# A partial tap sum and the layer norm's last mean read from PSUM instead of SBUF

## The chip, the cores and the metric

The kernel runs on one core of a Trainium2 chip. A time is the device time of one execution in microseconds (us), as the median of several runs. The engines are named as in the profile: PE is TensorE, DVE is VectorE, ACT is ScalarE, POOL is GpSimd, SP issues the loads. SBUF is the large on-chip memory, PSUM the small one of 8 banks (each 128 partitions by 512 f32) into which PE writes.

## The reference

A trunk of two layers on 512 tokens of 1024 channels, all in f32. The change lies in the second layer, a causal depthwise convolution followed by a layer norm:

```
u, g, xq, gate = split(h @ conv_w_in)               # 1536, 1536, 512, 2048 channels
glu = u * sigmoid(g)
y[t] = dw_b + sum over k of dw_w[k] * glu[t - 30 + k]   # 31 taps, per channel
y = silu(layernorm(y, ln_g, ln_b))                  # over the 1536 channels
x = x + rmsnorm((concat(y, memory_attention(xq)) * silu(gate)) @ conv_w_out) * norm_post_g
```

## The kernel before

Channels lie on the partitions and tokens on the free axis, so a tile is 128 channels by 512 tokens, and the convolution has 12 tiles (`NB`). Every product of the projections is done three times (high and low parts of both operands, lines 252 to 254, `split3`). The weights arrive in units of 128x1024: SP loads one into `wraw`, ACT casts it to `whi` (line 179), and DVE (line 183) or POOL (line 186, in two halves) subtracts to get the remainder `wlo`. Which of the two does it is fixed by the unit's number.

Every engine runs its instructions in the order in which the program emits them. `weave()` emits the chunks of a projection for PE and puts other work between them at given positions; it does not look at time. A product tile of u and g is left in two banks of the pool `mm` (4 banks); line 1037 takes the sigmoid on ACT and line 1038 multiplies on DVE into `gl`, which frees the banks for PE.

The taps: ahead of DVE's turn at a tile, ACT multiplies some of its taps (line 1063, into `pr`) and POOL sums them into `part` in SBUF (line 1064). That happens for 10 of the 12 tiles. DVE takes the remaining taps (line 1077), with the running sum in a PSUM bank of the pool `acc` (2 banks). Its first instruction for a tile multiplies `gl` by a tap and adds `part`; both tensors are in SBUF. The later ones add the bank `acc`. DVE works on two tiles in turn.

The layer norm: the mean of the first 8 tiles is taken off every tile early (line 1150). At the end `ln_sums` makes, on PE, the row of the sum of squares (line 1232) and the sum of the remaining differences on all partitions (line 1233); ACT scales the latter to a mean `es` in SBUF (line 1236); DVE makes the variance row (lines 1238, 1241) and takes `es` off the tiles (line 1247, `centre`): three tiles at once, the other nine one by one. PE turns the variance row into columns (line 1252), POOL takes the power -1/2 (lines 332, 335), DVE makes diagonals (line 340), PE spreads them (line 346). Then, per tile: centre, times the reciprocal deviation from PSUM (line 1267), silu on ACT (line 1268), times the gate (line 1274, both tensors in SBUF), high part on ACT (line 698), remainder on POOL (line 699). Two tiles make one of the units 2 to 7 of the output projection's first half, which PE runs meanwhile.

Of the kernel before, what the change touches and what calls it, by code (L numbers as in the profile page):

```python
# [58 lines left out]
def _turns(p):  # L59
    from fractions import Fraction  # L60

    # 1 / (2 pi) to 200 bits, by Machin's formula on integers
    one = 1 << 260

    def atan_inv(n):
        t = one // n
        s, k, sign = t, 3, -1
        while t:
            t //= n * n
            s += sign * (t // k)  # L70
            sign, k = -sign, k + 2
        return s

    pi = 4 * (4 * atan_inv(5) - atan_inv(239))
    f = Fraction((1 << p) * one, 2 * pi)
    f -= f.__floor__()
    if f > Fraction(1, 2):
        f -= 1
    c1 = round(f * 2**12) / 2.0**12
    r = f - Fraction(c1)  # L80
    c2 = round(r * 2**24) / 2.0**24
    c3 = float(r - Fraction(c2))
    q = 2.0**-p
    return c1 * q, c2 * q, c3 * q
# [7 lines left out]
def trunk(ctx, tc, x, x_t, mem_t, pos, g_cols, w_mem, post_g, w0, w1, dw_w, dw_b,  # L92
# [34 lines left out]
    ones = gp.tile([P, P], F32, name="ones")  # L127
    nhalf = gp.tile([P, 8], F32, name="nhalf")
# [9 lines left out]
    nc.gpsimd.memset(ones, 1.0)  # L138
    nc.gpsimd.dma_start(out=inv, in_=c_inv)
# [5 lines left out]
    # ------------------------------------------------------------------  # L145
    # weight stream: raw -> hi (float32r) and the exact remainder lo
    # ------------------------------------------------------------------
    units = [w_mem[i] for i in range(8)]
    units += [w0[i] for i in range(w0.shape[0])]
    # of the last product's second half, the first two units come early, then again  # L150
# [7 lines left out]
    def send(upto):  # L158
        """loads of the units before upto; a raw tile is free once its unit is split"""
        for i in range(sent["dma"], min(upto, sent["conv"] + 3, nu)):  # L160
            raws[i] = gp.tile([P, 2, G], F32, tag="wraw", bufs=3, name=nm("wraw"))
            src = units[i].rearrange("p (k c) -> p k c", k=2)
            for ks in (slice(0, 1), slice(1, 2)) if i == 0 else (slice(0, 2),):
                nc.sync.dma_start(out=raws[i][:, ks], in_=src[:, ks])
            sent["dma"] = i + 1
# [25 lines left out]
    def prefetch():  # L191
        """five split units at a time: those held, in use and ahead"""
        n = sent["use"]
        base = min(held) if held else n - 1
        conv_units(min(n + sent["ahead"], base + 5))
        send(sent["conv"] + 3)
# [14 lines left out]
    # ------------------------------------------------------------------  # L211
    # Every engine runs in the order of emission: weave() puts pieces of other work between
    # the chunks of a projection, where their operands are ready, and fill() work that only
    # other engines than the tensor engine do.
    # ------------------------------------------------------------------
# [40 lines left out]
    def proj(hT, tok_major, evac, n=S):  # L256
        """chunks of a group of 512 columns; evac(a, psum) as accumulator a is done"""
# [23 lines left out]
    def proj_halves(hT, evac, tok_major=False):  # L281
        """the same, the first half of the tokens before the second"""
# [37 lines left out]
    def rstd_two(ss):  # L320
        """of a row of D elements, from the sums of squares of its two halves"""
        v, w, r = tiny([P, 1]), tiny([P, 1]), tiny([P, 1])
        nc.gpsimd.tensor_scalar(out=v, in0=ss[:, 0:1], scalar1=1.0 / D, scalar2=EPS,
                                op0=ALU.mult, op1=ALU.add)
        nc.gpsimd.tensor_scalar(out=w, in0=ss[:, 1:2], scalar1=1.0 / D, scalar2=v,  # L325
                                op0=ALU.mult, op1=ALU.add)
        nc.gpsimd.tensor_tensor(out=r, in0=w, in1=nhalf[:, 0:1], op=ALU.pow)
        return r
# [15 lines left out]
    def spread(dg, sp):  # L344
        """column values -> the same along the free axis on every partition, from diags()"""
        nc.tensor.matmul(sp[:, :dg.shape[-1]], ones, dg, start=True, stop=True)
        return sp
# [11 lines left out]
    def split_T(pt, kp, gcol, dst):  # L359
        """transposed tiles (two of channels, two of tokens), times the gain, split"""  # L360
# [29 lines left out]
    # ------------------------------------------------------------------  # L390
    # start: loads ([channel, token]), warm-up of the tensor engine, memory keys and values
    # (the row scale of the memory's norm comes after the products)
    # ------------------------------------------------------------------
# [21 lines left out]
    def split_c(src, kp, gcol, dst):  # L415
        """channel tiles 2 kp and 2 kp + 1, times the gain, split"""
# [10 lines left out]
    def squares(key, xt):  # L427
        """of [channel, token], summed over the channel tiles"""
# [11 lines left out]
    def col_rstd(keys):  # L440
        """one column per tile of tokens"""
# [43 lines left out]
    # ------------------------------------------------------------------  # L485
    # memory attention: scores and softmax, transposes, gated output (split, [channel, token])
    # ------------------------------------------------------------------
    def xattn(xq, gx, yx, rs=None):
        """rs: what the scores of a token are scaled by, if not by SCALE alone"""
# [66 lines left out]
        def sides(at):  # L556
            """at[t]: chunks of the scores, the transposes and the output of tile t"""
# [8 lines left out]
    def part_of(sides, n):  # L566
        """those of group n of 16 chunks"""
        return [(pos_ - 16 * n, fn, cost) for pos_, fn, cost in sides if pos_ // 16 == n]
# [7 lines left out]
    # ------------------------------------------------------------------  # L576
    # output projection, post-norm and residual
    # ------------------------------------------------------------------
    def out_proj(yT, layer, res, finish, junk, sides, mids=()):
        """yT(j): split [channel, token] operand number j in stream order"""  # L580
# [4 lines left out]
        # the last tile of tokens ends with columns 512..767, then 768..1023, in two banks  # L585
# [118 lines left out]
    # ==================================================================  # L704
    # layer 0: retention
    # ==================================================================
    with tc.tile_pool(name="l0", bufs=1) as lp:
# [6 lines left out]
        def rope_tables():  # L714
            """in steps"""
# [15 lines left out]
            def rnd(o, i, scale):  # L731
                """nearest integer of i * scale"""
# [62 lines left out]
        # --- memory attention of layer 0 and the values, [token, channel]  # L795
# [4 lines left out]
        # the row scale of the norm comes after the products here as well  # L800
# [216 lines left out]
    # ==================================================================  # L1017
    # layer 1: convolution
    # ==================================================================
    with tc.tile_pool(name="l1", bufs=1) as lp:  # L1020
# [22 lines left out]
        # Taps 0..n-1 of a tile go to the scalar engine and GpSimd, which sum them ahead of the  # L1043
        # vector engine's turn; it then takes the others.
# [3 lines left out]
        def product():  # L1048
            """a tap on the scalar engine, summed by GpSimd; false if there is none to take"""
# [17 lines left out]
        def tap_sum(ct, k, first):  # L1067
            """a tap on the vector engine"""
            if first:
                accs[ct] = acc_ps()  # L1070
            gl, ac, tap = gls[ct], accs[ct], taps[:, ct, k:k + 1]
            o = cy[:, ct, :] if k == CW - 1 else ac
            if k == 0:
# [4 lines left out]
                out=o, in0=gl[:, k:k + S], scalar=tap,  # L1078
                in1=parts[ct] if first else ac, op0=ALU.mult, op1=ALU.add)

        def tap_sums(g):
            """the vector engine's turn at pair g"""
# [6 lines left out]
        def merge(a, b, stop=0.9):  # L1089
            """b spread over a, up to the fraction stop of it"""  # L1090
# [8 lines left out]
        # second half of the tokens of the layer's input, behind the first products  # L1099
# [12 lines left out]
        # Layer norm over channels (partitions and tiles).  The mean m0 of the first NM tiles  # L1112
        # serves as the shift: with d = y - m0 and e = mean(d), the centred d - e is what the
        # norm scales, and mean(d^2) - e^2 is its variance (e^2 is at most a third of mean(d^2),
        # as only 4 of 12 tiles can move the mean off m0).
# [3 lines left out]
        def gather(key, tile_):  # L1119
            """running sum on GpSimd"""  # L1120
# [108 lines left out]
        def ln_sums():  # L1229
            el, vr = tp_ps(), tp_ps()  # L1230
            for i, sq in enumerate([ln["dsums"]] + ln["sq"]):
                nc.tensor.matmul(vr[0:1, :], ones[:, 0:1], sq, start=i == 0, stop=i == 2)
            nc.tensor.matmul(el, ones, ln["d2"], start=True, stop=True)
            # var * BW = sum(d^2) - BW * e^2, as a row, then one column per tile of tokens
            es = ln["es"] = w2("m0", 1)
            nc.scalar.mul(out=es, in_=el, mul=1.0 / BW)
            e2 = w2("pr", PR)
            nc.vector.scalar_tensor_tensor(out=e2[0:1, :], in0=es[0:1, :], scalar=-float(BW),
                                           in1=es[0:1, :], op0=ALU.mult, op1=ALU.mult)
# [9 lines left out]
        def ln_cols():  # L1249
            vcol = tp_ps()  # L1250
# [42 lines left out]
        def norm_of(a, b):  # L1293
            """the steps of the norm that fall in chunks a..b-1 from the last gate's first"""
# [19 lines left out]
def _units(w, cols):  # L1314
    """[K, N] -> per group of 512 columns, per pair of K tiles: [128, 2 * 512]"""
# [61 lines left out]
```

## Time and profile before

| | |
|---|---|
| time, median of 3 runs | 844.36 us (843.94 to 844.42) |
| span of the profiled execution | 841.7 us |
| PE busy | 810.2 us, 96% |
| DVE busy | 526.8 us, 63% |
| POOL busy | 425.7 us, 51% |
| ACT busy | 347.7 us, 41% |

The profiled execution's own time is its span of 841.7 us; the median of the runs also holds what lies around the first and the last instruction, 2.7 us. Busy shares are means over the whole span: in the page's slices from about 505 to 715 us DVE is busy nine tenths of the time or more (the convolution). PE is the engine to look at first: 31.5 us of the span are without a matmul.

### The profile page before, as it was taken

To read this page: it belongs to the slowest core of one execution; us is meant where nothing else is said; L and a number is where in the kernel's file an instruction comes from. 1 tells how busy PE (TensorE), PEld (TensorE's weight loads), DVE (VectorE), ACT (ScalarE), POOL (GpSimd) and SP (SyncE) were. 2 spreads that over 40 slices of the span, in tenths; PEclk is the share of its full clock that TensorE was granted. 3 is DMA by queue.
4 is the path that set the end of the run, shared out by engine and by line. 5 is a ranking of instruction groups with operands and counts; after the bars stand their busy time and mean duration, and the time that the engine had idled before them with its cause. 6 is when DMAs were issued, how large, how long until landed. Compare 5 with 4: busy or idle time off the path is not lost.

```text
span 841.7 us, 10426 instructions
## 1 busy us (share of the span) xinstructions
PE 810.2 (96%) x3904; PEld 677.3 (80%) x3904; DVE 526.8 (63%) x814; ACT 347.7 (41%) x559; POOL 425.7 (51%) x380
## 2 busy tenths in 40 slices
PE   8999999999999999999999999979999989989897
PEld 8878888888888888888888988868877878766686
DVE  5797121143674642432337589999999999769523
ACT  6753356422112132332326352724678653335511
POOL 2145433356566564000043459988986898367101
PEclk9999999999999999999999999999999999999899
DMA  7722222222213112324423232222221124211522
GB/s 266 259 96 100 100 76 71 77 91 91 85 51 107 56 65 92 120 100 161 140 100 126 76 124 101 77 100 76 100 75 51 51 76 133 92 51 50 198 78 100
DMA packets 24961, 84.97 MB, mean 101 GB/s; under 512 B 2976, under 2 KB 4512, under 8 KB 24656
## 3 DMA queue, kind: packets, MB, share of 16 engines
q1 hardware_dynamic: 24256, 83.90, 28.8%
q8 instruction: 30, 0.49, 0.2%
q10 hardware_dynamic: 432, 0.21, 0.1%
q0 software_dynamic: 224, 0.21, 0.1%
q14 instruction: 19, 0.16, 0.1%
HBM read 80.11 MB, written 4.19 MB: 100 GB/s over the span
## 4 chain that ended last, share of the span: by engine, by line
PE 75%; DVE 14%; ACT 4%; DMA 3%; issue 2%; POOL 2%; SPq 0%; POOLq 0%; DVEq 0%; ACTq 0%
PE mm L252 21%; PE mm L253 21%; PE mm L254 21%; DVE acc L1077 6%; DMA wraw<-in_w_mem 2%; DVE cy L1274 1%; DVE cy L1247 1%; PE acc L919 1%; ACT whi L179 1%; PE tp L543 1%; PE tp L500 1%; DVE cy L1150 1%; DVE wlo L183 1%; PE tp L900 1%; PE acc L921 1%
## 5 line engine op out<-in xcount | busy, mean ns | idle before, releaser
L186 POOL TENSOR_TENSOR wlo<-wraw,whi 128x512 fp32r<-128x512 f32 x184 | 243.6, 1350 | 237.4 <-ACT whi L179 221.6
L252 PE MATMUL mm<-big,whi 128*128 128x512 f32 (+1 forms) x608 | 236.7, 389 | 10.3 <-DVE gl L1038 4.7
L254 PE MATMUL mm<-big,wlo 128*128 128x512 f32 (+1 forms) x608 | 229.2, 377 | 0.2 <-DVE wlo L176 0.2
L253 PE MATMUL mm<-big,whi 128*128 128x512 f32 (+1 forms) x608 | 228.9, 376 | 0.0
L1077 DVE SCALAR_TENSOR_TENSOR acc<-gl,taps,acc 128x512 f32<-128x512 f32 x282 | 188.5, 744 | 0.0
L179 ACT CAST whi<-wraw 128x1024 fp32r<-128x1024 f32 x133 | 137.1, 1047 | 89.6 <-PE mm L254 32.2
L254 PE MATMUL mm<-whi,big 128*128 128x512 f32 (+1 forms) x432 | 168.1, 389 | 2.0 <-POOL big L699 2.0
L252 PE MATMUL mm<-whi,big 128*128 128x512 f32 (+1 forms) x408 | 162.6, 398 | 0.0
L253 PE MATMUL mm<-wlo,big 128*128 128x512 f32 (+1 forms) x408 | 157.8, 387 | 0.2 <-DVE wlo L183 0.2
L252 PEld LDWEIGHTS mm<-big,whi 128*128 128x128 f32 x608 | 116.3, 191 | 31.1 <-DVE gl L1038 5.2
L254 PEld LDWEIGHTS mm<-big,wlo 128*128 128x128 f32 x608 | 116.2, 191 | 21.6 <-DVE wlo L176 0.6
L253 PEld LDWEIGHTS mm<-big,whi 128*128 128x128 f32 x608 | 116.2, 191 | 18.8 <-issue 0.5
L254 PEld LDWEIGHTS mm<-whi,big 128*128 128x128 f32 x432 | 81.5, 189 | 20.7 <-POOL big L699 3.9
L253 PEld LDWEIGHTS mm<-wlo,big 128*128 128x128 f32 x408 | 76.8, 188 | 15.5 <-DVE wlo L183 0.7
L252 PEld LDWEIGHTS mm<-whi,big 128*128 128x128 f32 x408 | 76.7, 188 | 14.5 <-issue 0.2
L183 DVE TENSOR_TENSOR wlo<-wraw,whi 128x1024 fp32r<-128x1024 f32 x41 | 54.5, 1344 | 41.9 <-ACT whi L179 41.8
L1064 POOL TENSOR_TENSOR part<-part,pr 128x512 f32<-128x512 f32 x56 | 72.5, 1317 | 6.1 <-ACT pr L1063 6.1
L892 ACT ACTIVATE kz<-tp,zeta 128x384 f32<-128x384 f32 x8 | 4.7, 584 | 96.5 <-PE tp L890 96.5
L1063 ACT ACTIVATE pr<-gl,taps 128x512 f32<-128x512 f32 x56 | 38.5, 717 | 1.8 <-POOL part L1064 1.8
L503 DVE TENSOR_REDUCE tiny<-tp 128x2 f32<-128x512 f32 x16 | 10.9, 684 | 27.0 <-PE tp L500 27.0
L325 POOL TENSOR_SCALAR tiny<-tiny,tiny 128x1 f32<-128x1 f32 x11 | 3.0, 271 | 41.1 <-ACT pr L600 34.6
L959 DVE TENSOR_TENSOR vb<-vb,ra 128x512 f32<-128x512 f32 x12 | 8.3, 691 | 24.0 <-ACT ra L957 24.0
(219 smaller groups left out, 904.1 us busy)
## 6 DMA issues: line engine op xcount, KB each, us to landing
wraw<-in_w SPq DMA_DIRECT2D x126, 512.0 KB, 3.3
wraw<-in_w_mem SPq DMA_DIRECT2D x7, 512.0 KB, 4.7
big<-in_x_t SPq DMA_DIRECT2D x2, 1024.0 KB, 7.5
o<-in_x SPq DMA_DIRECT2D x1, 2048.0 KB, 8.8
x1d<-o SPq DMA_DIRECT2D x4, 512.0 KB, 2.7
o<-x1d SPq DMA_DIRECT2D x1, 2048.0 KB, 10.2
out<-o SPq DMA_DIRECT2D x3, 512.0 KB, 2.6
big<-in_mem_t SPq DMA_DIRECT2D x4, 256.0 KB, 6.3
```

The costliest lines, as they stand in the source:

```text
L179: nc.scalar.copy(out=hi, in_=raw)
L183: nc.vector.tensor_tensor(out=lo, in0=raw, in1=hi.bitcast(F32), op=ALU.subtract)
L186: nc.gpsimd.tensor_tensor(out=lo[:, k], in0=raw[:, k], in1=hi[:, k].bitcast(F32), op=ALU.subtract)
L252: nc.tensor.matmul(dst, lh, rh, start=start, stop=False)
L253: nc.tensor.matmul(dst, lh, rl, start=False, stop=False)
L254: nc.tensor.matmul(dst, ll, rh, start=False, stop=stop)
L500: nc.tensor.matmul(sc[:, j * M:(j + 1) * M], xq[:, h, t * P:(t + 1) * P], mkT[:, h, :], start=True, stop=True)
L503: nc.vector.reduce_max(out=mx[:, hs], in_=sc.rearrange("p (a b) -> p a b", a=2), axis=AX.X)
L543: nc.tensor.matmul(po[:, h * P:(h + 1) * P], mv[:, m, h * P:(h + 1) * P], pT[:, m, h, :], start=m == 0, stop=m == 1)
L1063: nc.scalar.activation(out=pr, in_=gl[:, k:k + S], func=AF.Copy, scale=tap)
L1064: nc.gpsimd.tensor_tensor(out=parts[ct], in0=parts[ct], in1=pr, op=ALU.add)
L1077: nc.vector.scalar_tensor_tensor(out=o, in0=gl[:, k:k + S], scalar=tap, in1=parts[ct] if first else ac, op0=ALU.mult, op1=ALU.add)
```

## The change

Three edits. First, where a tile has a partial sum from POOL, a DVE copy of `part` into the tile's PSUM bank is put ahead of DVE's first tap, and that tap then adds the bank like all others. Second, the sum of differences is made with a matrix that holds 1/1536 instead of ones (`mean_of`, one more memset on POOL at the start), so PE writes the mean itself into PSUM; ACT's scaling of 128 rows becomes a copy of one row, needed because the variance uses the mean twice; `centre` reads the mean from PSUM. Third, the banks: the mean holds a bank of the pool `tp` (2 banks) until the last tile is centred, and the row of squares and the variance columns go to the pool `acc`. The diff also removes comments, which shifts line numbers.

```diff
+    mean_of = gp.tile([P, P], F32, name="mean_of")
...
     nc.gpsimd.memset(ones, 1.0)
+    nc.gpsimd.memset(mean_of, 1.0 / BW)
...
             if first:
                 accs[ct] = acc_ps()
+                if k:
+                    nc.vector.tensor_copy(out=accs[ct], in_=parts[ct])
...
             nc.vector.scalar_tensor_tensor(
-                out=o, in0=gl[:, k:k + S], scalar=tap,
-                in1=parts[ct] if first else ac, op0=ALU.mult, op1=ALU.add)
+                out=o, in0=gl[:, k:k + S], scalar=tap, in1=ac, op0=ALU.mult, op1=ALU.add)
...
         def ln_sums():
-            el, vr = tp_ps(), tp_ps()
+            es, vr = tp_ps(), acc_ps()
...
-            nc.tensor.matmul(el, ones, ln["d2"], start=True, stop=True)
-            es = ln["es"] = w2("m0", 1)
-            nc.scalar.mul(out=es, in_=el, mul=1.0 / BW)
-            e2 = w2("pr", PR)
+            nc.tensor.matmul(es, mean_of, ln["d2"], start=True, stop=True)
+            ln["es"] = es
+            e1, e2 = w2("m0", 1), w2("pr", PR)
+            nc.scalar.copy(out=e1[0:1, :], in_=es[0:1, :])
             nc.vector.scalar_tensor_tensor(out=e2[0:1, :], in0=es[0:1, :], scalar=-float(BW),
-                                           in1=es[0:1, :], op0=ALU.mult, op1=ALU.mult)
+                                           in1=e1[0:1, :], op0=ALU.mult, op1=ALU.mult)
...
         def ln_cols():
-            vcol = tp_ps()
+            vcol = acc_ps()
```

On DVE, where its turn at the second pair of tiles with a partial sum begins (`part` is POOL's sum, `acc` the PSUM bank, `gl` the gated input), the order before is:

```order
L1077 SCALAR_TENSOR_TENSOR cy<-gl_4038,taps,acc_4270 128x512
L1077 SCALAR_TENSOR_TENSOR acc_4590<-gl_4211,taps,part_4274 128x512
L1077 SCALAR_TENSOR_TENSOR acc_4592<-gl_4234,taps,part_4292 128x512
L1038 TENSOR_TENSOR gl_4600<-mm_4435,gl_4600 128x512
L1077 SCALAR_TENSOR_TENSOR acc_4590<-gl_4211,taps,acc_4590 128x512
```

And at the same place with the change:

```order
L1081 SCALAR_TENSOR_TENSOR cy<-gl_4040,taps,acc_4272 128x512
L1074 COPY acc_4594<-part_4278 128x512
L1081 SCALAR_TENSOR_TENSOR acc_4594<-gl_4213,taps,acc_4594 128x512
L1074 COPY acc_4597<-part_4296 128x512
L1081 SCALAR_TENSOR_TENSOR acc_4597<-gl_4236,taps,acc_4597 128x512
L1040 TENSOR_TENSOR gl_4606<-mm_4439,gl_4606 128x512
```

Two copies come in; the multiply that frees PE's banks (line 1038, now 1040) stays behind both first taps.

On DVE in the layer norm, from the variance row on (`m` is the mean in SBUF, `tp` a PSUM bank), before:

```order
L1238 SCALAR_TENSOR_TENSOR pr_6040<-m_1020_6038 1x512
L1241 TENSOR_TENSOR pr_6042<-tp_6033,pr_6040 1x512
L1247 TENSOR_TENSOR cy<-cy,m_1020_6038 128x512 x3
L1255 COPY tiny_6071<-tp_6066 128x4
L340 TENSOR_SCALAR pr_6103<-ident,tiny_6075 128x128 x4
L1267 TENSOR_TENSOR cy<-cy,tp_6108 128x512 x2
L1274 TENSOR_TENSOR cy<-cy,big_5353 128x512
```

And with the change:

```order
L1241 SCALAR_TENSOR_TENSOR pr_6051<-tp_6044,m_1020_6050 1x512
L1244 TENSOR_TENSOR pr_6054<-acc_6045,pr_6051 1x512
L1250 TENSOR_TENSOR cy<-cy,tp_6044 128x512 x3
L1258 COPY tiny_6083<-acc_6078 128x4
L342 TENSOR_SCALAR pr_6115<-ident,tiny_6087 128x128 x4
L1270 TENSOR_TENSOR cy<-cy,tp_6120 128x512 x2
L1277 TENSOR_TENSOR cy<-cy,big_5363 128x512
```

Nothing moves here; the operands change their memory.

## Rows read from the trace of the kernel before

**Rows 1.** Waits of PE, whole span: us in total, times, longest us

```profile
PE mm L252 <- DVE gl L1038: 4.7, 1, 4.7
PE mm L252 <- ACT whi L179: 3.3, 1, 3.3
PE mm L252 <- ACT big L1217: 2.8, 1, 2.8
PE tp L346 <- DVE pr L340: 2.7, 1, 2.7
PE mm L254 <- POOL big L699: 2.0, 3, 0.7
...
PE mm L253 <- DVE wlo L183: 1.6, 2, 1.3
```

**Rows 2.** Stretches of PE: from:to, us, busy (matmuls), granted clock, DMA

```profile
567.00:572.20 5.20, 5.17 (x12) 0.51 0.01 3
572.20:580.00 7.80, 7.80 (x36) 1.00 0.19 67
746.35:753.00 6.65, 6.64 (x20) 0.76 0.23 79
783.50:788.00 4.50, 4.42 (x12) 0.59 0.67 204
```

**Rows 3.** DVE's groups by form: count, busy us, mean ns, idle before

```profile
L1077 DVE SCALAR_TENSOR_TENSOR acc<-gl,taps,acc 128x512 f32<-128x512 f32 x282 | 188.5, 744 | 0.0
...
L1077 DVE SCALAR_TENSOR_TENSOR acc<-gl,taps,part 128x512 f32<-128x512 f32 x10 | 18.6, 1886 | 1.0 <-POOL part L1064 1.0
L1247 DVE TENSOR_TENSOR cy<-cy,m 128x512 f32<-128x512 f32 x12 | 13.5, 1137 | 0.0
...
L1267 DVE TENSOR_TENSOR cy<-cy,tp 128x512 f32<-128x512 f32 x12 | 8.1, 686 | 2.5 <-PE tp L346 2.2
```

**Rows 4.** Line 1077's instructions: shortest/median/longest ns, first and last start

```profile
L1077 DVE SCALAR_TENSOR_TENSOR acc<-gl,taps,part x10: 747/1415/5464, 521.7 to 693.4; 128x512 f32<-128x512 f32 x10
```

**Rows 5.** Timeline of DVE in the taps: start us, us, line, operation

```profile
559.25 7.13 DVE L1077 SCALAR_TENSOR_TENSOR acc<-gl,taps,part 128x512 f32<-128x512 f32 x2 [1.04 <-POOL part L1064]
...
642.85 0.98 DVE L1077 SCALAR_TENSOR_TENSOR acc<-gl,taps,part 128x512 f32<-128x512 f32 x1
...
644.43 1.08 DVE L1077 SCALAR_TENSOR_TENSOR acc<-gl,taps,part 128x512 f32<-128x512 f32 x1
```

**Rows 6.** Timeline of POOL at the first of these

```profile
560.43 2.51 POOL L186 TENSOR_TENSOR wlo<-wraw,whi 128x512 fp32r<-128x512 f32 x2
562.91 2.92 POOL L1128 TENSOR_TENSOR sum<-sum,cy 128x512 f32<-128x512 f32 x2
```

**Rows 7.** Timeline of DVE, a single-input instruction from SBUF to PSUM

```profile
475.35 0.81 DVE L1074 TENSOR_SCALAR acc<-gl,taps,cvec 128x512 f32<-128x512 f32 x1
```

**Rows 8.** Timeline of POOL at that time

```profile
475.53 11.31 POOL L186 TENSOR_TENSOR wlo<-wraw,whi 128x512 fp32r<-128x512 f32 x9 [11.39 <-ACT whi L179]
```

**Rows 9.** Line 340's instructions, single-input from SBUF to SBUF

```profile
L340 DVE TENSOR_SCALAR pr<-ident,tiny x4: 275/779/1297, 743.4 to 746.0; 128x128 f32<-128x128 f32 x4
```

**Rows 10.** Timeline of DVE in the layer norm

```profile
737.72 1.87 DVE L1247 TENSOR_TENSOR cy<-cy,m 128x512 f32<-128x512 f32 x3
...
743.41 2.89 DVE L340 TENSOR_SCALAR pr<-ident,tiny 128x128 f32<-128x128 f32 x4 [3.75 <-POOL tiny L335]
748.47 1.28 DVE L1267 TENSOR_TENSOR cy<-cy,tp 128x512 f32<-128x512 f32 x2 [2.17 <-PE tp L346]
...
751.85 1.79 DVE L1247 TENSOR_TENSOR cy<-cy,m 128x512 f32<-128x512 f32 x1
...
777.89 1.92 DVE L1274 TENSOR_TENSOR cy<-cy,g 128x512 f32<-128x512 f32 x2
```

**Rows 11.** Timeline of POOL in the layer norm

```profile
737.31 4.68 POOL L186 TENSOR_TENSOR wlo<-wraw,whi 128x512 fp32r<-128x512 f32 x2 [4.53 <-ACT whi L179]
...
751.47 3.31 POOL L699 TENSOR_TENSOR big<-cy,big 128x512 fp32r<-128x512 f32 x2 [5.64 <-ACT big L698]
```

## Prediction

> **What bounds the kernel now.** I read the busy shares first: TensorE (PE) has work for 810.2 of 841.7 us, so a change pays only where it shortens one of TensorE's waits or the slow stretch behind one. The list of TensorE's waits is therefore the second view [rows 1]. In the convolution layer five matter: 4.7 us until VectorE's multiply at line 1038 frees two banks; 2.7 us at the spreading matmul of the layer norm; 3.3 us on a weight cast and 1.3 us on a weight remainder late in the norm; 2.0 us in three pieces on GpSimd's remainders; and 2.8 us on a gate's evacuation. Third come the stretches behind these waits [rows 2]. [...]
>
> Fourth, why VectorE is late. Grouped by form, a tap that adds a PSUM bank takes 744 ns, the one that adds `part` from SBUF 1886; centring with the mean in SBUF takes 1137 ns, the equally large multiply that reads PSUM 686 [rows 3]. The ten `part` taps run from 747 to 5464 ns [rows 4], so the size isn't the cost, the moment is. Their timeline says which moment: at 559.25 two of them last 7.13 us together [rows 5] while GpSimd runs four SBUF additions back to back [rows 6]. VectorE's instructions with two SBUF inputs and GpSimd's SBUF instructions exclude each other; the other side of it is GpSimd's pair at 737.31, which takes 4.68 us instead of 2.51 while VectorE centres three tiles [rows 6, 10, 11].
>
> [...]
>
> **The change, part by part.** *The first taps.* Ten copies come in, and ten taps lose their second SBUF input. A copy isn't in the trace. Its nearest rows are the 128x512 multiply with a PSUM operand, 0.69 us [rows 3], and a one-input instruction from SBUF to PSUM, 0.81 us with GpSimd at work beside it [rows 7, 8]. At the other end it waits as the tap did, 1.14 us more on average and up to 4.7 [rows 3, 4]; a one-input instruction from SBUF to SBUF does wait (275 to 1297 ns for 128x128) [rows 9]. Less than 0.69 has no support in any row, so I exclude it. I take 0.69, since row 7 has the copy's memories and no wait. Per tile 0.69 + 0.74 replaces 1.89: 0.45 less, 4.5 us less VectorE time over ten.
>
> VectorE time is not TensorE time. The gain lies at 559 us. There copy, tap, copy, tap take 2.9 us instead of 7.13, so line 1038 comes 4.2 us earlier, and some more since POOL gets its next operands sooner (ACT may refill `part` as soon as the copy has read it). TensorE's 4.7 us shrink to about 0.2: **4.5 us**. [...] Against this: at the other pairs the wait was short (0.98 and 1.08 us at 643 [rows 5]), and copy plus tap there takes 2 x 1.43, about 0.8 us more. VectorE is without slack there, and the gate evacuation for which TensorE waits 2.8 us [rows 1] is behind it on ACT, after a VectorE multiply: that wait grows by **0.8 us**. The pair after that ends well before TensorE asks for the sums, so it costs nothing.
>
> *Start of the norm.* The mean's matmul has the same size; the copy of one row has as many elements per partition as the scaling it replaces; the variance row reads one PSUM operand instead of none. I cost these at nothing. If the PSUM reads were slower, each 0.1 us would be on the path. The three centrings no longer hold up GpSimd's pair at 737.31, so it ends at about 739.8 instead of 742.0 [rows 11]. Behind it in GpSimd's queue stands the power that gives the deviations, and then line 340's diagonals, which VectorE starts at 743.41 after 3.75 us of waiting [rows 10]. They come 2.2 us earlier; TensorE's 2.7 us become 0.5: **2.2 us**. The 20 matmuls behind it take 6.65 us; at 0.217 they would take 4.3, but the spreading matmul has more passes than the others, so I take **1.6 us** of the 2.3. That cover is thin: the next GpSimd pair still contends with the diagonals, as now.
>
> *The tiles of the norm.* Now VectorE goes from 751.85 to 779.81, 27.96 us, for tiles 3 to 11, with a wait both at centring and at the gate multiply. With the mean in PSUM only the gate multiply has two SBUF inputs. It alternates with one GpSimd instruction: 1.25 us (half of 2.51) plus 0.62 (a third of 1.87), and centring and scaling, 2 x 0.62, fit beside the 1.25 [rows 6, 10]. Ten gate multiplies at 1.87 are 18.7 us, 9.3 less. With the earlier start of 3.4 us (2.2, and a spreading matmul at full clock), the last one ends about 12.7 us earlier. What hangs on it: ACT's weight casts stand behind the last tile's cast, and VectorE's line 183 behind the last gate multiply; for these TensorE waits 3.3 and 1.3 us. TensorE gets there only some 4 us earlier, so the 4.6 us vanish with about 4 to spare (12.7 - 4 - 4.6): **4.6 us**. The 12 matmuls at the slow level behind it cost 4.50 - 2.6: **1.9 us**.
>
> What is late next is GpSimd: its 12 remainders and 4 halves of weight units still run in turn with the gate multiplies, and TensorE, which starts this part earlier, meets the first four remainders sooner than GpSimd delivers them. Now these waits are 2.0 us; I estimate 3.2 from 1.87 us per GpSimd step: **-1.2 us**.
>
> [...]
>
> *The banks.* The mean's bank in `tp` is next wanted by the last tile of the output projection, far behind. The two banks of `acc` are wanted by TensorE a few matmuls behind the spreading; the variance row and columns were read before that, the columns at about 739.7. No wait. The extra memset comes after the ones that TensorE's warm-up waits for: nothing.
>
> **Sum.** 4.5 + 2.6 - 0.8 + 2.2 + 1.6 + 4.6 + 1.9 - 1.2 = 15.4 us off a span of 841.7, so 826.3, and with the 2.7 us around it **829.0 us** against 844.36.
>
> **Rivals.**
> 1. [...] The gate multiply loses its turn several times in a row, as the tap did at 559. For it: rows 4 and 5. Against: at 751.85 centring waited for one GpSimd instruction only (1.79 us), though another stood ready. Then the last gate multiply ends about as late as now less 3.4; the weight waits stay and only the start's 3.8 us remain: 844.4 - 6.3 - 3.8 = 834.3.
> 2. *The tap gain is given back before the norm.* TensorE runs ahead of VectorE, which is busy throughout, and waits longer at the gate evacuation than 0.8. For it: VectorE's full slices. Against: behind 559 VectorE itself moves forward with TensorE. If half of the 7.1 goes: 844.4 - 15.4 + 3.5 = 832.5.
> [...]
> 4. [...] Every GpSimd instruction must be waited for by some VectorE instruction, so the copies wait as the taps did and the gate multiplies inherit what centring waited. [...] It decides once a copy takes over 1.2 us on average (then copy plus tap exceed 1.89). Against: the 282 bank taps don't wait at all.
>
> **How the numbers follow.** Forecast 60%, rival 1 15%, rival 2 13%, rival 3 8%, rival 4 4%. The forecast's own range: 4.7 + 2.6 whole and all of the norm's waits (another 4 us) gives 824.5; a norm that keeps half of its late waits gives 832. The range 824 to 835 takes in rivals 1 and 2 and leaves out 3 and 4 and the edge of the forecast. A measurement here can tell 0.2%, 1.7 us, from no change. Faster by more: forecast and rivals 1 to 3, less a little for an unforeseen wait: 0.94; within 0.2%: 0.02; slower: 0.04.
>
> **What would show it.** Right: copies near 0.69 us with no spread, all taps near 744 ns, no wait of TensorE on line 1038, no slow stretch after it; GpSimd's pair in the norm's start near 2.5 us; centrings near 0.69 us; gate multiplies up to 1.9 us; no wait on the weight cast behind the last tile; waits on GpSimd's remainders somewhat larger. Wrong: copies with a long tail, gate multiplies of several us, a new wait of TensorE on `acc`, or a gate evacuation wait that has grown by as much as the first wait lost.

## The result and the profile after

The changed kernel takes 831.63 us (median of 4 runs, 830.01 to 831.99) against 844.39 for the kernel before beside it: a ratio of 0.9845 with a 95% interval of 0.9831 to 0.9859, so 12.8 us saved where 15.4 were forecast. The span of its profiled execution is 829.8 us, 11.9 less than before. Line numbers have shifted by 1 to 4 (the weight cast 179 is now 181, the gate multiply 1274 is 1277).

TensorE's waits (us in total, times, longest) answer to [rows 1]:

```profile
PE mm L254 <- ACT whi L181: 3.3, 1, 3.3
PE mm L254 <- ACT whi L177: 2.6, 1, 2.6
PE mm L255 <- DVE wlo L185: 2.5, 2, 1.6
PE mm L254 <- ACT big L1220: 2.4, 1, 2.4
...
PE tp L348 <- DVE pr L342: 0.7, 1, 0.7
PE mm L256 <- POOL big L701: 0.5, 2, 0.3
```

The 4.7 us on the multiply that frees the banks are gone, the spreading matmul waits 0.7 instead of 2.7, the remainders 0.5 instead of 2.0, the gate evacuation 2.4 instead of 2.8. The wait on the late weight cast is what it was, 3.3 us, and the one on the weight remainder behind it has grown from 1.3 to 1.6. (The 2.6 us on line 177 are at the kernel's start; they were 2.1 before, and the change is not near them.)

Stretches of TensorE (from:to, us, busy (matmuls), granted clock, DMA share, GB/s), to be read against [rows 2]:

```profile
559.00:570.00 11.00, 11.00 (x51) 1.00 0.14 49
...
736.50:739.50 3.00, 2.60 (x10) 1.00 0.56 180
...
771.00:775.00 4.00, 4.00 (x10) 0.50 0.70 213
```

The convolution around the first wait of before and the norm's start now run at a granted clock of 1.00. The 6.65 us behind the spreading wait of [rows 2] have become 5.06:

```profile
736.90:741.96 5.06, 5.06 (x21) 1.00 0.33 107
```

The third stretch above is the one behind the late weight wait: 10 matmuls in 4.00 us at a granted clock of 0.50, where the stretch of before has 12 in 4.50 at 0.59 [rows 2].

VectorE, grouped by form (busy us, mean ns | idle before), beside [rows 3]:

```profile
L1081 DVE SCALAR_TENSOR_TENSOR acc<-gl,taps,acc 128x512 f32<-128x512 f32 x292 | 195.7, 747 | 0.4
...
L1277 DVE TENSOR_TENSOR cy<-cy,big 128x512 f32<-128x512 f32 x8 | 10.9, 1367 | 0.3 <-ACT cy L1271 0.3
...
L1250 DVE TENSOR_TENSOR cy<-cy,tp 128x512 f32<-128x512 f32 x12 | 7.9, 673 | 0.0
L1074 DVE COPY acc<-part 128x512 f32<-128x512 f32 x10 | 6.8, 684 | 0.2 <-POOL part L1066 0.2
```

and the copies' line by itself (shortest/median/longest ns, first and last start), beside [rows 4]:

```profile
L1074 DVE COPY acc<-part x10: 674/684/694, 522.3 to 687.4; 128x512 f32<-128x512 f32 x10
```

The copies take 684 ns with hardly any spread, though GpSimd is at work beside eight of the ten; centring takes 673 instead of 1137. But the gate multiply, the one instruction of the norm's tiles that still has two SBUF inputs, has become slower. In the kernel before it read:

```profile
L1274 DVE TENSOR_TENSOR cy<-cy,big 128x512 f32<-128x512 f32 x8 | 8.3, 1034 | 0.3 <-ACT cy L1268 0.3
```

So on average 333 ns of the 464 that a centring lost came back on a gate multiply of this form. Where the nine tiles spend their time is seen in VectorE's timeline after the change (start us, us), beside [rows 10]:

```profile
741.41 0.68 DVE L1250 TENSOR_TENSOR cy<-cy,tp 128x512 f32<-128x512 f32 x1
...
745.69 1.72 DVE L1277 TENSOR_TENSOR cy<-cy,big 128x512 f32<-128x512 f32 x1
...
748.65 1.71 DVE L1277 TENSOR_TENSOR cy<-cy,big 128x512 f32<-128x512 f32 x1
...
751.60 1.34 DVE L1277 TENSOR_TENSOR cy<-cy,big 128x512 f32<-128x512 f32 x1
...
754.18 1.34 DVE L1277 TENSOR_TENSOR cy<-cy,big 128x512 f32<-128x512 f32 x1
...
765.26 1.93 DVE L1277 TENSOR_TENSOR cy<-cy,g 128x512 f32<-128x512 f32 x2
```

and GpSimd's at the same time, beside [rows 11]:

```profile
729.86 2.52 POOL L188 TENSOR_TENSOR wlo<-wraw,whi 128x512 fp32r<-128x512 f32 x2 [6.17 <-ACT whi L181]
...
743.87 2.99 POOL L188 TENSOR_TENSOR wlo<-wraw,whi 128x512 fp32r<-128x512 f32 x2
746.83 2.99 POOL L701 TENSOR_TENSOR big<-cy,big 128x512 fp32r<-128x512 f32 x2
751.10 1.30 POOL L701 TENSOR_TENSOR big<-cy,big 128x512 fp32r<-128x512 f32 x1 [1.28 <-ACT big L700]
753.67 1.29 POOL L701 TENSOR_TENSOR big<-cy,big 128x512 fp32r<-128x512 f32 x1 [1.28 <-ACT big L700]
```

The chain goes from 741.41 to 767.19 (765.26 + 1.93), 25.78 us where it was 27.96: 2.2 saved, not 9.3. Two spacings occur between the gate multiplies from the third (742.73) on, five of the first kind and three of the second. Where GpSimd has work in hand (745.69 to 748.65) a tile takes 2.96 us, the time of two GpSimd instructions. The first of these has centring and scaling beside it, but the gate multiply comes up 0.1 us too late: GpSimd's second weight half (the second of the two at 743.87, here by itself) has just begun.

```profile
745.58 1.28 POOL L188 TENSOR_TENSOR wlo<-wraw,whi 128x512 fp32r<-128x512 f32 x1
```

Where GpSimd has none (751.60 to 754.18) a tile takes 2.58, and GpSimd itself idles 1.28 of it: the remainder at 751.10 waits for ScalarE's high part, and that for the gate multiply before it. The remainder then lasts to 752.40, and the gate multiply that stood ready at 751.60 is through at 752.94.

### The profile page after: what moved, and what is told of

It is laid out like the page before. It is cut to its first block, busy times and chain, and to the rows that moved or that the text cites. A ratio compares the mean times of both kernels' runs of the same rounds, so it can differ in the third digit from the quotient of the medians.

```text
span 829.8 us, 10432 instructions
## 1 busy us (share of the span) xinstructions
PE 806.1 (97%) x3904; PEld 674.9 (81%) x3904; DVE 520.1 (63%) x824; ACT 347.8 (42%) x559; POOL 417.5 (50%) x381
## 4 chain that ended last, share of the span: by engine, by line
PE 76%; DVE 14%; ACT 4%; DMA 3%; POOL 1%; issue 1%; SPq 0%; POOLq 0%; DVEq 0%; ACTq 0%
PE mm L254 22%; PE mm L255 22%; PE mm L256 22%; DVE acc L1081 5%; DMA wraw<-in_w_mem 2%; DVE cy L1277 2%; PE acc L921 1%; DVE wlo L185 1%; ACT whi L181 1%; PE tp L545 1%; PE tp L502 1%; DVE cy L1153 1%; PE tp L902 1%; PE acc L923 1%; DVE cy L1270 1%
## 5 line engine op out<-in xcount | busy, mean ns | idle before, releaser
L188 POOL TENSOR_TENSOR wlo<-wraw,whi 128x512 fp32r<-128x512 f32 x184 | 239.1, 1324 | 234.0 <-ACT whi L181 225.1
L1081 DVE SCALAR_TENSOR_TENSOR acc<-gl,taps,acc 128x512 f32<-128x512 f32 x292 | 195.7, 747 | 0.4
L1039 ACT ACTIVATE gl<-mm 128x512 f32<-128x512 f32 x12 | 7.2, 599 | 38.5 <-PE mm L256 38.5
```

Of the source, the lines that this page charges most:

```text
L188: nc.gpsimd.tensor_tensor(out=lo[:, k], in0=raw[:, k], in1=hi[:, k].bitcast(F32), op=ALU.subtract)
L1081: nc.vector.scalar_tensor_tensor(out=o, in0=gl[:, k:k + S], scalar=tap, in1=ac, op0=ALU.mult, op1=ALU.add)
```

## Experiments

The theory (A) after this result: both parts work by sparing VectorE's instructions the waits that they have, with two SBUF inputs, beside GpSimd's SBUF instructions (1886 ns for a first tap and 1137 for a centring, on average [rows 3], where a bank tap now takes 747 and a centring 673); they add; in the norm the gate multiply then waits for the remainder that has begun just before it, and that keeps the late weight wait. Where an expectation calls this a port that an instruction holds, the name is the author's: the runs show the waits, and not what lies behind them. Rivals came with each run.

**Each part alone.** The kernel before with the copies and the bank as the first tap's operand:

```diff
+                if k:
+                    nc.vector.tensor_copy(out=accs[ct], in_=parts[ct])
...
-                in1=parts[ct] if first else ac, op0=ALU.mult, op1=ALU.add)
+                in1=ac, op0=ALU.mult, op1=ALU.add)
```

> Only the copies of the partial sums; the layer norm is the one of before. Theory A (the two parts add up, each by its own wait): the span of the changed kernel stands 7.5 to 8.0 us ahead at the end of the convolution, so 844.4 - 8.0 = 836.4 us, and the norm's part keeps its old lengths (TensorE waits 2.7 us at the spreading matmul). Theory B (the tap gain would be given back where TensorE waits for VectorE later, and only the two edits together pay): 839 us or more, with a longer wait at the gate evacuation.

And the changed kernel without these lines:

> Only the layer norm's mean from PSUM; the first taps read the partial sum from SBUF as before. Theory A: 4.5 us less, 839.9 us: the wait at the spreading matmul and the slow stretch after it go (about 3.5 us), the waits on the late weight unit stay at some 5 us. Theory B (the norm gains only when TensorE comes earlier): 842 us or more. The first taps keep their tail of up to 5 us.

Measured: the taps alone 836.83 us, ratio 0.9906 (0.9892 to 0.9919), 8.0 less than the 844.8 beside it; the norm alone 840.78, ratio 0.9952 (0.9939 to 0.9964), 4.0 less. Together 12.0, and the whole change gave 12.8: they add, within what these runs can tell. TensorE's waits in the run with the norm alone show the two sorts side by side, the wait at 559 whole, the late weight wait whole, the spreading wait down to 0.7 us:

```profile
PE mm L254 <- DVE gl L1040: 4.7, 1, 4.7
PE mm L254 <- ACT whi L181: 3.3, 1, 3.3
...
PE mm L255 <- DVE wlo L185: 2.5, 2, 1.6
...
PE tp L348 <- DVE pr L342: 0.7, 1, 0.7
```

So the tap part gave more than its 6.3 us, and the norm less than half of its 9.1.

**Remainders off GpSimd.** In the changed kernel the twelve remainders of the norm's tiles go to VectorE, one tile later:

```diff
-            split_y(ym[c], j, z, nc.gpsimd)
+            nc.scalar.copy(out=ym[c][0][j], in_=z)
+        def z_lo(ct):
+            c, j = ct // 4, ct % 4
+            nc.vector.tensor_tensor(out=ym[c][1][j], in0=cy[:, ct, :], in1=ym[c][0][j].bitcast(F32),
+                                    op=ALU.subtract)
...
+            if ct > 1:
+                z_lo(ct - 2)
+            if ct == NB:
+                z_lo(NB - 1)
```

> The changed kernel, with the 12 remainders of the norm's tiles on VectorE, one tile later, instead of GpSimd. Theory A (the gate multiply waits because a GpSimd remainder holds the port when it comes up): the gate multiplies fall from a mean of 1.37 us to about 0.7 except beside the two GpSimd pairs of weight remainders; VectorE's cycle per tile becomes four instructions of 0.62 us, 2.5 us, about the 2.6 to 3.0 of now, so the time stays within 2 us of 831.6. Theory B (the gate multiply waits for ScalarE's silu or for its gate): they stay above 1.3 us, and the time rises by the 12 x 0.62 us of added VectorE work, to 836 or more.

Measured: 832.01 us, ratio 0.9843 (0.983 to 0.9857), no gain over the change. What it was to test is the gate multiplies (VectorE's timeline):

```profile
742.60 1.77 DVE L1277 TENSOR_TENSOR cy<-cy,big 128x512 f32<-128x512 f32 x1
747.27 0.68 DVE L1277 TENSOR_TENSOR cy<-cy,big 128x512 f32<-128x512 f32 x1
...
752.32 0.68 DVE L1277 TENSOR_TENSOR cy<-cy,big 128x512 f32<-128x512 f32 x1
754.84 1.80 DVE L1277 TENSOR_TENSOR cy<-cy,big 128x512 f32<-128x512 f32 x1
```

Without GpSimd's remainders they take 0.68 us; the two long ones stand beside GpSimd's two weight units. That the 1.3 to 1.7 us are waits for GpSimd's instructions is thereby shown. VectorE has four instructions a tile instead, 2.52 us, and TensorE waits 4.7 us for the remainders, which now stand in VectorE's queue, so nothing is won.

**Remainders started at the right moment.** They stay on GpSimd, but from the third on each waits, by a one-element read, for the gate multiply of the next tile, so that it runs beside centring and scaling (`z_lo` as above, on GpSimd):

```diff
+            if ct in (1, 2):
+                z_lo(ct - 1)
+            if ct > 3:
+                nc.gpsimd.tensor_copy(out=tiny([P, 1]), in_=cy[:, ct - 1, 0:1])
+                z_lo(ct - 2)
+            if ct == NB:
+                z_lo(NB - 1)
```

> The changed kernel, but in the norm's tiles each of GpSimd's remainders from the third on waits, through a one-element read on GpSimd, for the gate multiply of the next tile, so that it starts where a gate multiply ends and has centring and scaling (which read PSUM) beside it. Theory A (a gate multiply waits for the GpSimd instruction that began just before it): gate multiplies from tile 4 on fall from about 1.4 to 0.7-0.9 us, the spacing from 2.57-2.96 to about 2.1 us, the last gate multiply ends some 3 us earlier (about 764 instead of 767.2), TensorE's late wait on the weight cast falls from 3.3 to about 2 us or less, time 827 to 830. Rival B (GpSimd and VectorE together are saturated here, so order can't win): the spacing stays above 2.5 us, 831 or more.

Measured: 826.34 us, ratio 0.9773 (0.9759 to 0.9786), 5.3 us less than the change's 831.63, or 6.1 by the two ratios, each taken against the kernel before beside it. Its profile comes from one more run of the same kernel:

> The kernel of the run whose remainders start behind a gate multiply, once more, for a profile (its five times had a median of 826.34). Theory A: gate multiplies from tile 4 on near 0.7-0.9 us at a spacing of about 2.05 us, the last one ends at about 763.5, TensorE's wait on the weight cast behind the last tile is under 2 us, time 826 to 827. Rival: gate multiplies still above 1.3 us, and the gain comes from elsewhere.

It took 826.93 us. Its VectorE and GpSimd timelines:

```profile
748.98 0.82 DVE L1277 TENSOR_TENSOR cy<-cy,big 128x512 f32<-128x512 f32 x1
...
751.04 0.78 DVE L1277 TENSOR_TENSOR cy<-cy,big 128x512 f32<-128x512 f32 x1
...
762.90 1.42 DVE L1277 TENSOR_TENSOR cy<-cy,g 128x512 f32<-128x512 f32 x1 [0.28 <-ACT cy L1271]
```

```profile
749.87 0.18 POOL L1301 COPY tiny<-cy 128x1 f32<-128x1 f32 x1 [0.61 <-DVE cy L1277]
750.00 1.27 POOL L1290 TENSOR_TENSOR big<-cy,big 128x512 fp32r<-128x512 f32 x1
```

The remainder starts at 750.00, right after a gate multiply (748.98 + 0.82), and is over at 751.27, as the next gate multiply begins. The spacing is 2.06 us. Four gate multiplies still wait (1.42 to 1.72 us): one behind the first two remainders, which nothing holds back, two beside weight units, and the last one. The last gate multiply ends at 764.32 instead of 767.19, and TensorE's list has no wait on the weight cast any more:

```profile
PE mm L256 <- POOL big L1290: 2.6, 4, 1.1
...
PE mm L255 <- DVE wlo L185: 1.1, 1, 1.1
```

The price is that each remainder comes later for TensorE (2.6 us in four waits instead of 0.5). The theory holds: the same work, with each remainder begun one gate multiply later, takes a fifth less per tile where no weight unit is beside it.

**Weight units earlier.** If the chain can't be shortened, the cast that waits behind it can be put ahead of it:

```diff
+        sent["ahead"] = 4
```

stands ahead of the output projection, where units were cast three ahead.

> The changed kernel, with the weight units of the last projection split one unit further ahead (four instead of three), so that the cast of the unit for which TensorE waits stands between the norm's tiles in the queues of ScalarE and VectorE and not behind them. Theory A (the wait of 3.3 + 1.6 us is the place in the queue): it falls below 2 us, part of it comes back at the next unit, and the time is 3 to 5 us less, 827 to 829 us. Theory B (the wait is really for the tiles of the norm or for the loads): it moves whole to the next unit or to the tiles, 831 to 833 us.

Measured: 829.8 us, ratio 0.9821 (0.9808 to 0.9835), 1.8 less than the change. The late weight wait went and a new one came, 2.9 us on the last norm, because in ScalarE's queue casts that wait for their loads now stand ahead of the sums of squares:

```profile
774.93 1.05 ACT L181 CAST whi<-wraw 128x1024 fp32r<-128x1024 f32 x1 [3.64 <-DMA wraw<-in_w]
777.24 1.04 ACT L181 CAST whi<-wraw 128x1024 fp32r<-128x1024 f32 x1 [1.25 <-DMA wraw<-in_w]
778.19 0.59 ACT L602 ACTIVATE pr<-mm 128x512 f32<-128x512 f32 x1
```

The next kernel goes back to three ahead in time, and another has both remedies, this one and the later remainders:

```diff
+        sent["ahead"] = 4
-                 norm_of(16, 99))
+                 norm_of(16, 99) + [(13, lambda: sent.update(ahead=3))])
```

> The run with weight units cast four ahead of TensorE, but back to three ahead from chunk 13 of the output projection on. Theory A (the 2.9 us that TensorE then waited for the last norm, line 622, came from casts that waited for their loads ahead of the sums of squares in ScalarE's queue): that wait goes to under 1 us and the late weight wait stays gone: 826 to 828.5. Rival B (the wait only moves back to a later weight unit): 829.5 or more, with a TensorE wait of 2 us or more on a cast or a remainder.

> Both edits of the two runs before: remainders that start behind a gate multiply, and weight units cast four ahead up to chunk 13. If the late weight wait is one wait which each of them takes off, they don't add: 825.5 to 828, at most 1 us under the better of the two. If each removes waits of its own (remainders here, casts there), they add: below 825.5.

Measured: 826.97 us, ratio 0.978 (0.9767 to 0.9794), with the wait on the last norm down to 0.6; and both remedies 826.59, ratio 0.9772 (0.9759 to 0.9786). They don't add: it is one wait, and either takes it off. All three versions beat the change by about 5 us (5.5 to 6.2 by the ratios), and can't be told apart.

**Which copies the taps need.** The kernel before, with the copy for the one pair of tiles at 559:

```diff
+            seed = first and k and ct in (4, 5)
...
+                if seed:
+                    nc.vector.tensor_copy(out=accs[ct], in_=parts[ct])
...
-                in1=parts[ct] if first else ac, op0=ALU.mult, op1=ALU.add)
+                in1=parts[ct] if first and not seed else ac, op0=ALU.mult, op1=ALU.add)
```

> The kernel before, with the copy put ahead of the first tap for two of the ten tiles alone, the pair whose first taps took 7.13 us together. Theory A (the tap edit's gain is that one place: TensorE's wait on the gated input's multiply and the slow stretch behind it): 835.5 to 837.5, like the run with all ten copies (836.8); TensorE's wait of 4.7 us is gone. Rival B (the gain is VectorE time saved at all ten tiles, 0.45 us each): one fifth of it, 841 or more.

Measured: 842.3 us, ratio 0.996 (0.9946 to 0.9974). Theory A is wrong here, and so is the rival: the time lies where it put it, but 3.6 us are saved against the 845.91 beside it, of the 8.0 that ten copies save, and not one fifth of them; nor is its reason the right one. The wait at 559 did go (TensorE waits 0.7 us there in place of 4.7). It came up again 35 us later. VectorE:

```profile
561.17 0.69 DVE L1073 COPY acc<-part 128x512 f32<-128x512 f32 x1 [1.09 <-POOL part L1064]
...
595.77 5.57 DVE L1080 SCALAR_TENSOR_TENSOR acc<-gl,taps,part 128x512 f32<-128x512 f32 x2
```

GpSimd, and TensorE behind it:

```profile
592.78 2.56 POOL L1064 TENSOR_TENSOR part<-part,pr 128x512 f32<-128x512 f32 x2
595.28 2.56 POOL L186 TENSOR_TENSOR wlo<-wraw,whi 128x512 fp32r<-128x512 f32 x2
597.78 3.01 POOL L1131 TENSOR_TENSOR sum<-sum,cy 128x512 f32<-128x512 f32 x2
```

```profile
618.22 2.04 PE L500 MATMUL tp<-mkT,big 128*128 128x256 f32 x8 [1.98 <-ACT w L514]
625.91 0.66 PE L536 MATMUL tp<-ident,w 128*128 128x128 f32 x4 [1.53 <-ACT w L514]
```

In the kernel before, this pair came at 599.94 and took 2.61 us, with the last two instructions of GpSimd's run coming up:

```profile
599.94 2.61 DVE L1077 SCALAR_TENSOR_TENSOR acc<-gl,taps,part 128x512 f32<-128x512 f32 x2
```

```profile
600.25 3.44 POOL L1128 TENSOR_TENSOR sum<-sum,cy 128x512 f32<-128x512 f32 x2
```

There each tap waited for one GpSimd instruction. Having won time at 559, VectorE arrives 4.2 us earlier, with one GpSimd instruction more still to come. Its first tap gets in only after three of them, ahead of the last, and the second waits for that last one (the run ends at 600.79, the taps at 601.34). The maxima for the memory attention stand behind them on VectorE, and TensorE waits for the softmax. So a next run with the copies for this pair too:

> The kernel before with the copy for four tiles, the pair of the run before (whose profiled execution lost at the next pair, at 595.77, what the copies had won: two first taps took 5.57 us there, before 2.61, and TensorE waited 2.0 and 1.5 us for the softmax behind them) and that next pair. Theory C (the wait of VectorE's two-SBUF tap moves to the next such tap that meets a run of GpSimd additions, and ends at the pairs where GpSimd leaves gaps): with both pairs on copies the gain holds, no first tap over 2 us behind them, 836 to 838. Rival D (the wait moves on once more, to the pair at about 643): first taps there take over 4 us together, TensorE's gate evacuation wait grows, 840 or more.

Measured: 839.23 us, ratio 0.993 (0.991 to 0.995), a little above what theory C gave, and below the two-tile run, though the two intervals touch. The first taps of the next pair take 0.99 and 1.08 us there, so the wait doesn't move on. That this is because GpSimd leaves gaps, as theory C has it, isn't shown: GpSimd runs on there without one. With 2, 4 and 10 copies the kernel saves 0.4, 0.7 and 0.9%; the gap between 4 and 10 is within the intervals.

**Is it the form of the instruction?** A tap lost several turns in a row (5.46 us at 559.25), a gate multiply loses one (1.34 to 1.73 us). The changed kernel with the gate multiply as the tap's instruction:

```diff
-            nc.vector.tensor_tensor(out=z, in0=z, in1=gates[c][j], op=ALU.mult)
+            nc.vector.scalar_tensor_tensor(out=z, in0=z, scalar=1.0, in1=gates[c][j],
+                                           op0=ALU.mult, op1=ALU.mult)
```

> The changed kernel with the twelve gate multiplies as SCALAR_TENSOR_TENSOR (the form of a tap, times 1.0 first) instead of TENSOR_TENSOR; same operands, same memories. Open is why a tap at 559 lost several turns against GpSimd in a row (5.46 us) while a gate multiply loses one (1.34 to 1.73 us). If the form decides: gate multiplies that meet GpSimd work back to back (the first from tile 3 on) take more than 2.5 us, the chain of nine tiles grows beyond 28 us, time 834 or more. If the situation decides (what GpSimd has ready): they stay at 1.34 to 1.73 us, chain 25 to 26 us, time 831 to 833.

Measured: 830.47 us in one run (842.92 for the kernel before beside it). The multiplies are as they were:

```profile
L1277 DVE SCALAR_TENSOR_TENSOR cy<-cy,big 128x512 f32<-128x512 f32 x8 | 11.0, 1370 | 0.3 <-ACT cy L1271 0.3
```

So it isn't TENSOR_TENSOR against SCALAR_TENSOR_TENSOR that decides. The run doesn't cover the whole form of a tap, which reads its scalar from SBUF (here it is the constant 1.0) and writes PSUM (here SBUF). But the taps at 599.94 have that form whole and lost one turn each, so the form alone can't be the reason.

## Why the prediction was right, and where it was not

The time fell inside the range and on the right side. That it came within 2.6 us of the forecast is in part luck: the taps gave 8.0 us where 6.3 were counted, the norm 4.0 to 4.5 where 9.1 were, and the two errors have opposite signs. Two of the three places came out; the third did not, and the first was worth more than its terms.

- *First taps.* The copy at 0.69 us: measured 0.684, and no wait, so rival 4 falls as far as the copies go. TensorE's 4.7 us and the slow stretch behind them went, as forecast (4.5 and 2.6): the 2.6 are the 5.20 us of the 12 matmuls at 0.51 less 12 x 0.217, and 0.217 is 7.80 us by 36 at 1.00 [rows 2]; with the change 51 took 11.00 us at 1.00, 0.216 each. The term of -0.8 was wrong in sign: the gate evacuation wait shrank by 0.4 and the attention's waits at line 538 (536 before) by 0.6. By ScalarE's evacuation of the last four gates (from 722.46 us before, 715.01 after) the kernel is 7.45 us ahead, or 8.0 counted from a start that was 0.5 later; forecast were 6.3, and the taps alone gave 8.0.
- *Why the working there was incomplete all the same.* It said that the gain lies at 559 and costed the other pairs by how long they waited in the kernel before. The run with two copies shows that this is not how such a wait behaves: alone, the cure at 559 saves 0.4%, since 3.0 us are lost at the next pair (5.57 against 2.61), which had waited little. The copies at the other tiles, priced as a loss, keep the gain.
- *Start of the norm.* Forecast 2.2 and 1.6; the spreading wait fell by 2.0, since GpSimd's pair took 2.52 us instead of 4.68, and the stretch behind it ran at 1.00 and took 1.6 less. The spreading matmul, one in the program and two records in the trace, still took 593 and 667 ns there at 1.00 (1061 and 1222 before), the ones from 738.06 on 390 to 400. Right.
- *Tiles of the norm: the step that failed.* It said that gate multiply and GpSimd instruction alternate, 1.25 + 0.62, with centring and scaling beside the 1.25. Both halves of that are off. Where GpSimd has work in hand, it does go on at once, but centring and scaling, counted as 2 x 0.62 = 1.24, take 1.31 us to the start of the gate multiply (744.38 to 745.69). GpSimd has then begun its next instruction 0.1 us before, so two of them go by for each tile: 2.96, in five spacings of eight. Where it has none, it can't begin at the moment a gate multiply ends: the remainder needs ScalarE's high part of that very product, so it begins 0.73 us later (751.60 + 1.34 = 752.94 to 753.67), and the next gate multiply comes up in the middle of it: 1.87 + 0.7 = 2.57, as measured. The chain gave 2.2 us instead of 9.3, so the 4.6 and 1.9 us at the weight wait stayed. The chain's end and TensorE each moved forward by 12.6 us (779.81 to 767.19; 778.19 to 765.55), so the distance between them is what it was. The later remainders, which bring the spacing near the forecast one (2.06 for 1.87; the nine tiles take 22.6 us, from 741.75 to 764.32, for 18.7), took this wait off and gave 5.3 us: much of the gain was there to be had, but not in this order of events.
- *Remainders.* Forecast -1.2; the waits fell from 2.0 to 0.5. Why they are delivered sooner no run isolates; nearest is that centring no longer holds GpSimd up. With this the norm gave 4.5 in all.
- *Rivals.* Rival 1 had the weight waits stay, as they did, but by gate multiplies that lose several turns; they lost one each. Its 834.3 becomes 832.6 with the 8.0 us that the taps gave, so the time of 831.6 doesn't speak against it; the trace does. Rival 2 didn't happen. Rival 4 was right on one point: the gate multiplies inherited much of what centring had waited (333 of 464 ns). The PSUM operand costs nothing that can be seen: the first three centrings take 1.86 us together (from 730.18 on) where they took 1.87 from SBUF.

## What to carry to other kernels

Where one engine's instructions wait for another's, as first taps of 747 to 5464 ns did here, cost a cure by what meets what afterwards, not by the wait that the trace shows: here the wait moved to the next instructions with two SBUF inputs, from 559 to 595 us and from centring to the gate multiply. Cure the next such places too and look again (four tiles kept what two had lost), or set the other engine's start so that its work lies beside instructions that showed no such wait (here centring and scaling from PSUM, 0.67 to 0.69 us). And before two engines are put down as alternating, look for what starts the second one and how much room is left beside it: a link through a third engine (here 0.73 us of ScalarE), or 0.1 us too much work, decided here whether they interlock.

## What the runs showed that was not expected

- A VectorE instruction with two SBUF inputs lost to several GpSimd instructions in a row. Of the 7.13 us for two taps at 559.25, the first tap took 5.46: four GpSimd instructions went by before it got in, ahead of the fifth, and the second tap waited for that one. At 595.77 in the run with two copies it was three and one (5.57 us for the two). The gate multiplies lost one turn each (1.34 to 1.73 us), and so did the taps at 599.94 (2.61 us for the two), so the instruction's form alone is not the reason; what is stays open. The first tap and the fifth instruction by themselves:

```profile
559.25 5.46 DVE L1077 SCALAR_TENSOR_TENSOR acc<-gl,taps,part 128x512 f32<-128x512 f32 x1 [1.04 <-POOL part L1064]
```

```profile
564.24 1.59 POOL L1128 TENSOR_TENSOR sum<-sum,cy 128x512 f32<-128x512 f32 x1
```

- Copying from SBUF to PSUM took 674 to 694 ns in all ten cases, eight of them beside GpSimd at work.
- A cure can be made on GpSimd's side at almost no cost: a one-element read of 0.18 us that only holds it back won as much as casting weights earlier (826.34 us against 826.97).
